# Who subtracts the low part of an expert's weights: VectorE with a GpSimd share, or VectorE alone

## The chip, the cores and the metric

The program runs on one core of a Trainium2 chip. Its engines are TensorE (matmuls, PE in the profile; its weight loads are PEld), VectorE (DVE), ScalarE (ACT), GpSimd (POOL) and SyncE (SP, which here only issues transfers). The metric is the device time of one execution in microseconds (us). A difference of about 0.3% (some 11 us) is what a measurement of this kernel can tell from no change.

## The reference

Two transformer blocks over 512 tokens of width 1024, all in fp32. The first block ends in a mixture of 32 experts, of which each token uses four:

```python
def expert_block(args):
    tok_b, e = args
    xb = h[tok_b]
    u = xb @ w1[e] + b1[e]                       # w1[e]: 1024 x 2048
    glu = jnp.minimum(u[:, 0::2], SWIGLU_LIMIT)
    lin = jnp.clip(u[:, 1::2], -SWIGLU_LIMIT, SWIGLU_LIMIT)
    act = glu * jax.nn.sigmoid(SWIGLU_ALPHA * glu) * (lin + 1.0)
    return act @ w2[e] + b2[e]                   # w2[e]: 1024 x 1024
```

All 32 experts' weights are read once: 32 x 12 MB. The second block (attention layers) takes the rest of the program and has no experts.

## The kernel before, in words

**The expert stage** takes the span from about 800 to 2390 us. An expert's weights are read in 24 pieces: 16 of `w1` (four column blocks of 512, by four pairs of row blocks) and 8 of `w2`. A piece `wraw` is 128 partitions x 1024 fp32 (two row blocks of 512 columns), 512 KB, loaded by one transfer that SP issues (L1312).

**Hi and lo.** A piece reaches TensorE in the type fp32r, as two parts that together keep fp32's precision: ScalarE copies it into `whi` as fp32r (L1324), and `wlo` = `wraw` - `whi` is the low part. The subtraction is divided by columns: of the 1024 columns VectorE does the first 736 (L1328) and GpSimd the last 288 (L1329); `q = 288` stands in `Weights.split`. Both need the finished `whi`, each reads two tensors in SBUF, and they need nothing of each other. Then TensorE uses both parts: for each of the two row blocks `x*hi` (L1706), `x*lo` (L1707) and, for blocks of 128 rows, `x_low*hi` (L1709). TensorE's L1707 waits until both engines have written their columns. The nine experts with a capacity of exactly 128 rows are not split (`whole(r)`): their pieces go to TensorE raw, as plain fp32 (L1702).

**Buffers.** There are seven `wraw` buffers and four of each of `whi` and `wlo`. A raw buffer comes free when ScalarE, VectorE and GpSimd have read it (or TensorE, of a whole expert), and SP then issues the next load into it, in order. `Weights.ahead` keeps the loads and splits ahead of `Weights.next`, which hands TensorE its next piece.

**What else runs on the two engines.** For each 512-column block of `w1` the function `swiglu` evicts the sums: for experts of 64 rows ScalarE copies half of them (L1717), VectorE adds the halves (L1718), clamps them (L1724, L1725), ScalarE makes the sigmoid (L1726), VectorE and GpSimd multiply (L1727, L1728), and TensorE transposes the result `ln` (L1687). GpSimd also issues the gathers of token rows (L1674), and close to the end of the stage multiplies the four accumulators by a gate (L1877, 128 x 1024 each), before VectorE adds the residual (L1878).

**The order.** Each engine runs its instructions in the order in which the program states them, and they wait for each other by semaphores. `order(g)` writes out by hand how the column blocks of three or four experts of different sizes follow each other.

**The other stages.** `split` serves the output projection before the experts with the same object. The second block makes a `Weights` object of its own (L3084).

Of the kernel before, what the change touches and what calls it, by code (L numbers as in the profile page):

```python
# [8 lines left out]
F = mybir.dt.float32  # L9
# [3 lines left out]
OP = mybir.AluOpType  # L13
# [85 lines left out]
class Blk1:  # L99
    def __init__(self, tc, ins, ctx, ident, ones, ps, dram):  # L100
        self.tc, self.nc, self.i, self.ps, self.dram = tc, tc.nc, ins, ps, dram
        self.ident, self.ones, self.ctx = ident, ones, ctx
        self.c = ctx.enter_context(tc.tile_pool(name="f1c", bufs=1, side="right"))
# [1150 lines left out]
def whole(r):  # L1254

    return CAP[r] == 128
# [32 lines left out]
class Rows:  # L1289


    def __init__(self, tiles, n, split):
        self.tiles, self.n, self.split = tiles, n, split


class Weights:


    def __init__(self, tc, ctx, raw=7, parts=4, kn=2, side="left"):
        self.tc, self.nc, self.kn = tc, tc.nc, kn  # L1300
        self.nraw, self.nsplit = raw, parts - 1
        self.raw = ctx.enter_context(tc.tile_pool(name="wraw", bufs=raw, side=side, reuse_waits="tile"))
        self.par = ctx.enter_context(tc.tile_pool(name="wpar", bufs=parts, side=side, reuse_waits="tile"))
# [12 lines left out]
    def split(self, raw, room=None):  # L1316
        nc = self.nc
        raw, n = raw
        hi, lo = room or [self.par.tile([128, self.kn, 512], R, name="w" + a) for a in ("hi", "lo")]
        if n < 512:  # L1320
            nc.scalar.activation(hi[:, :, :n], raw[:, :, :n], AF.Copy)
            nc.vector.tensor_tensor(lo[:, :, :n], raw[:, :, :n], hi[:, :, :n].bitcast(F), op=OP.subtract)
            return hi, lo
        nc.scalar.activation(hi, raw, AF.Copy)  # L1324
        q = 288
        rw, hw, lw = (t.rearrange("p k n -> p (k n)") for t in (raw, hi, lo))
        m = 512 * raw.shape[1] - q
        nc.vector.tensor_tensor(lw[:, :m], rw[:, :m], hw[:, :m].bitcast(F), op=OP.subtract)  # L1328
        nc.gpsimd.tensor_tensor(lw[:, m:], rw[:, m:], hw[:, m:].bitcast(F), op=OP.subtract)  # L1329
        return hi, lo  # L1330

    def stream(self, parts):
# [42 lines left out]
class Moe:  # L1375
# [301 lines left out]
    def rows_tiles(self, name, n, split=True, bufs=None):  # L1677
        m = 2 if n == 128 and split else 1
        return Rows([self.x.tile([128, 8, 128], R if split else F, name=name, tag=name, bufs=bufs or self.tbufs) for _ in range(m)], n, split)
# [104 lines left out]
    def experts(self, hD, x1, gt2):  # L1784
        nc, x_, c, I = self.nc, self.x, self.c, self.i
        self.tbufs, self.abufs, self.gbufs = 5, 6, 2
        kn = self.W.kn
        idxf, idx, gate, prepare = self.idxf, self.idx, self.gatec, self.prepare
        seq = sequence()
# [3 lines left out]
        def blocks(r):  # L1793
            return [(r, 0, min(CAP[r], 128))] + ([(32 + r, 128, 64)] if CAP[r] > 128 else [])
# [136 lines left out]
        for r in ranks:  # L1931
            m = sum(2 if b[2] == 128 and not whole(r) else 1 for b in blocks(r))
# [1176 lines left out]
```

## Time and profile before

| | us |
|---|---|
| median of 3 runs | 3789.82 (3784.77 to 3796.57) |
| the profiled execution, its own time | 3795.27 |
| its span, first to last instruction | 3793.5 |

| engine | busy in the whole span |
|---|---|
| PE | 3424.3 us, 90% |
| DVE | 2510.3 us, 66% |
| POOL | 1734.7 us, 46% |
| ACT | 1696.9 us, 45% |

The busy time of a matmul is modelled from its start, so a busy PE can still lose time. In the tables of waits, a row names the instruction that sat waiting, what ended its wait, the sum of such idle time, how often, and the longest. The granted clock is the share of TensorE's full 2.4 GHz: 1.00, or 0.50 (1.2 GHz) in stretches.

### The profile page before, as it was taken

The numbers are of one execution on the slowest core, as the hardware profiler recorded it, in microseconds if no ns is written. First come the engines' busy times: TensorE is split into PE (matmuls) and PEld (weight loads), VectorE is DVE, ScalarE is ACT, GpSimd is POOL, SyncE is SP. The second block draws the span as 40 slices with busy tenths as digits, with TensorE's granted clock in tenths as the row PEclk, the third lists the DMA queues.
The fourth block names the chain that finished last, engine by engine and source line by source line (L and its number), as shares of the span: only waits on it lengthen the run. The fifth ranks groups of instructions, "written<-read, shape, count | busy, mean of one in ns | idle before, by whom it ended". The sixth has DMA issues, their size and how long they took to land. (4 is left out here: it accounts for less than half of the span.)

```text
span 3793.5 us, 51274 instructions
## 1 busy us (share of the span) xinstructions
PE 3424.3 (90%) x16864; PEld 2510.5 (66%) x16864; DVE 2510.3 (66%) x4793; ACT 1696.9 (45%) x2937; POOL 1734.7 (46%) x1509
## 2 busy tenths in 40 slices
PE   7966679769898999999899989799999999999999
PEld 4756567645565565656465655488878878887887
DVE  7778875667786787766786856754566445546653
ACT  4634323224555555545555544444434434343442
POOL 4444333435665666555675755433342342334223
PEclk9976677869899999999999989899999999999999
DMA  7853243627778888877878788532221243223113
GB/s 255 265 141 83 65 104 92 211 98 249 248 234 276 290 285 279 263 263 262 295 258 294 239 273 290 174 90 75 74 85 51 61 140 101 79 73 84 40 51 106
DMA packets 420649, 653.86 MB, mean 172 GB/s; under 512 B 83939, under 2 KB 145568, under 8 KB 419862
## 3 DMA queue, kind: packets, MB, share of 16 engines
q1 hardware_dynamic: 414650, 633.32, 52.2%
q0 software_dynamic: 4000, 13.90, 1.2%
q10 hardware_dynamic: 1724, 3.28, 0.3%
q8 instruction: 135, 2.21, 0.2%
q14 instruction: 140, 1.15, 0.1%
HBM read 610.80 MB, written 39.61 MB: 171 GB/s over the span
## 5 line engine op out<-in xcount | busy, mean ns | idle before, releaser
L1329 POOL TENSOR_TENSOR wlo<-wraw,whi 128x288 fp32r<-128x288 f32 x736 | 957.3, 1311 | 1001.7 <-ACT whi L1324 935.2
L1328 DVE TENSOR_TENSOR wlo<-wraw,whi 128x736 fp32r<-128x736 f32 x736 | 828.5, 1133 | 472.4 <-ACT whi L1324 458.5
L1324 ACT ACTIVATE whi<-wraw 128x1024 fp32r<-128x1024 f32 x736 | 769.9, 1056 | 609.8 <-DMA wraw<-in_w 193.3
L2275 PE MATMUL psg<-whi,xh 128*128 128x512 f32 (+1 forms) x1152 | 472.4, 410 | 0.3 <-ACT xh L2292 0.3
L2277 PE MATMUL psg<-whi,xl 128*128 128x512 f32 (+1 forms) x1152 | 451.2, 392 | 0.0
L2276 PE MATMUL psg<-wlo,xh 128*128 128x512 f32 (+1 forms) x1152 | 449.7, 391 | 0.0
L1707 PE MATMUL ps<-wlo,x 128*128 128x512 f32 x928 | 383.7, 413 | 29.9 <-DVE wlo L1328 25.6
L1706 PE MATMUL ps<-whi,x 128*128 128x512 f32 x928 | 393.6, 424 | 1.0 <-ACT whi L1324 0.8
L1702 PE MATMUL ps<-wraw,x 128*128 128x512 f32 x576 | 277.4, 634 | 0.0
L2277 PEld LDWEIGHTS psg<-whi,xl 128*128 128x128 f32 x1152 | 217.5, 189 | 42.3
L1728 POOL TENSOR_TENSOR ln<-ln,sg 64x256 f32<-64x256 f32 (+1 forms) x152 | 166.5, 1096 | 163.9 <-DVE ln L1727 107.7
L2275 PEld LDWEIGHTS psg<-whi,xh 128*128 128x128 f32 x1152 | 218.1, 189 | 35.0 <-ACT xh L2292 1.5
L2276 PEld LDWEIGHTS psg<-wlo,xh 128*128 128x128 f32 x1152 | 218.3, 189 | 34.5
L1707 PEld LDWEIGHTS ps<-wlo,x 128*128 128x128 f32 x928 | 179.4, 193 | 91.9 <-DVE wlo L1328 44.7
L1706 PEld LDWEIGHTS ps<-whi,x 128*128 128x128 f32 x928 | 179.5, 193 | 72.1 <-issue 23.3
L1707 PE MATMUL ps<-wlo,a 128*128 128x512 f32 x464 | 195.8, 422 | 8.9 <-DVE wlo L1328 4.8
L1702 PEld LDWEIGHTS ps<-wraw,x 128*128 128x128 f32 x576 | 111.9, 201 | 136.2 <-issue 135.3
L1706 PE MATMUL ps<-whi,a 128*128 128x512 f32 x464 | 195.1, 421 | 1.5 <-ACT whi L1324 1.4
L2415 ACT ACTIVATE pexp<-pss,mx 128x128 f32<-128x128 f32 x192 | 101.0, 527 | 154.7 <-DVE mx L2410 66.6
L1726 ACT ACTIVATE sg<-gl 64x256 f32<-64x256 f32 (+1 forms) x152 | 62.9, 414 | 168.6 <-DVE gl L1724 153.6
L1702 PE MATMUL ps<-wraw,a 128*128 128x512 f32 x288 | 138.3, 619 | 0.0
L1707 PEld LDWEIGHTS ps<-wlo,a 128*128 128x128 f32 x464 | 90.6, 195 | 47.8 <-DVE wlo L1328 16.4
(736 smaller groups left out, 6927.8 us busy)
## 6 DMA issues: line engine op xcount, KB each, us to landing
wraw<-in_w SPq DMA_DIRECT2D x768, 512.0 KB
wraw<-in_w_in SPq DMA_DIRECT2D x140, 512.0 KB
mraw<-in_w_ada SPq DMA_DIRECT2D x32, 512.0 KB
wraw<-in_w_out SPq DMA_DIRECT2D x24, 512.0 KB
wada<-in_w_ada SPq DMA_DIRECT2D x16, 512.0 KB
wraw<-in_w_mem_kv SPq DMA_DIRECT2D x16, 512.0 KB
wraw<-in_w_branch_m SPq DMA_DIRECT2D x8, 512.0 KB
wraw<-in_w_branch_b SPq DMA_DIRECT2D x8, 512.0 KB
```

The source lines that it names most:

```text
L1324: nc.scalar.activation(hi, raw, AF.Copy)
L1328: nc.vector.tensor_tensor(lw[:, :m], rw[:, :m], hw[:, :m].bitcast(F), op=OP.subtract)
L1329: nc.gpsimd.tensor_tensor(lw[:, m:], rw[:, m:], hw[:, m:].bitcast(F), op=OP.subtract)
L1702: nc.tensor.matmul(ps, a, w[:, k], start=s, stop=e)
L1706: nc.tensor.matmul(ps, a, hi[:, k], start=s, stop=False)
L1707: nc.tensor.matmul(ps, a, lo[:, k], start=False, stop=e and not two)
L1726: nc.scalar.activation(sg[:m], gl[:m], AF.Sigmoid, scale=1.702)
L1728: nc.gpsimd.tensor_tensor(ln[:m], ln[:m], sg[:m], op=OP.mult)
L2275: nc.tensor.matmul(p, xh[:, kk], hi[:, k, :n], start=kk == 0, stop=False)
L2276: nc.tensor.matmul(p, xh[:, kk], lo[:, k, :n], start=False, stop=False)
L2277: nc.tensor.matmul(p, xl[:, kk], hi[:, k, :n], start=False, stop=kk == kch - 1)
L2415: nc.scalar.activation(p[:, :n], s[:, :n], AF.Exp, bias=nm, scale=-1.0, accum_out=H["d"][:, i:i + 1])
```

## The change

The 288 columns become an attribute of the class, and the expert stage sets it to zero for its own object. VectorE's instruction then covers all 1024 columns and GpSimd's is not issued. Everything else stays: the same loads, the same copy on ScalarE, the same matmuls. The output projection before it and the second block keep 288.

```diff
 class Weights:
+    share = 288
+
     def __init__(self, tc, ctx, raw=7, parts=4, kn=2, side="left"):
...
         nc.scalar.activation(hi, raw, AF.Copy)
-        q = 288
+        q = self.share
         rw, hw, lw = (t.rearrange("p k n -> p (k n)") for t in (raw, hi, lo))
         m = 512 * raw.shape[1] - q
         nc.vector.tensor_tensor(lw[:, :m], rw[:, :m], hw[:, :m].bitcast(F), op=OP.subtract)
-        nc.gpsimd.tensor_tensor(lw[:, m:], rw[:, m:], hw[:, m:].bitcast(F), op=OP.subtract)
+        if q:
+            nc.gpsimd.tensor_tensor(lw[:, m:], rw[:, m:], hw[:, m:].bitcast(F), op=OP.subtract)
         return hi, lo
...
     def experts(self, hD, x1, gt2):
         nc, x_, c, I = self.nc, self.x, self.c, self.i
         self.tbufs, self.abufs, self.gbufs = 5, 6, 2
+        self.W.share = 0
         kn = self.W.kn
```

## Rows read from the trace of the kernel before

**Rows 1.** The page, busy time and share of the span by engine.
```profile
PE 3424.3 (90%) x16864; PEld 2510.5 (66%) x16864; DVE 2510.3 (66%) x4793; ACT 1696.9 (45%) x2937; POOL 1734.7 (46%) x1509
```
**Rows 2.** Busy time by stretch: us, engines' busy (count), granted clock, DMA share, GB/s.
```profile
800.00:2390.00 1590.00, 1463.78 (x5296) 917.87 (x5296) 1142.34 (x1667) 828.20 (x1147) 948.06 (x772) 0.94 0.79 263
...
1300.00:1400.00 100.00, 89.41 (x301) 53.10 (x301) 74.65 (x94) 56.47 (x77) 65.08 (x52) 0.93 0.87 296
...
1473.00:1483.00 10.00, 9.42 (x16) 4.68 (x17) 5.12 (x11) 3.96 (x8) 2.84 (x4) 0.50 0.98 336
```
**Rows 3.** Waits of TensorE's matmuls, expert stage: sum us, times, longest us.
```profile
PE ps L1687 <- POOL ln L1728: 56.8, 19, 6.8
PE ps L1707 <- DVE wlo L1328: 30.4, 39, 3.5
PE ps L1687 <- DMA xg<-hD,idxi: 19.1, 7, 4.2
PE ps L1707 <- POOL wlo L1329: 7.0, 12, 1.1
```
**Rows 4.** Waits of TensorE's weight loads, same stage.
```profile
PEld ps L1707 <- DVE wlo L1328: 61.1, 77, 4.0
...
PEld ps L1707 <- POOL wlo L1329: 24.9, 47, 1.6
```
**Rows 5.** Groups by line and form, same stage: busy us, mean ns | idle before.
```profile
L1329 POOL TENSOR_TENSOR wlo<-wraw,whi 128x288 fp32r<-128x288 f32 x548 | 710.3, 1309 | 407.5 <-ACT whi L1324 376.0 <-PE ps L1707 9.8 <-PE ps L1702 7.8
L1328 DVE TENSOR_TENSOR wlo<-wraw,whi 128x736 fp32r<-128x736 f32 x548 | 621.7, 1144 | 273.6 <-ACT whi L1324 261.2 <-PE ps L1707 7.4 <-PE ps L1706 1.4
...
L1728 POOL TENSOR_TENSOR ln<-ln,sg 64x256 f32<-64x256 f32 x92 | 113.7, 1236 | 82.1 <-DVE ln L1727 44.0 <-PE ps L1702 19.7 <-PE ps L1707 4.2
...
L1724 DVE TENSOR_SCALAR gl<-us 64x256 f32<-64x256 f32 x92 | 54.0, 587 | 0.8
...
L1877 POOL TENSOR_TENSOR acc<-acc,gtr 128x1024 f32<-128x1024 f32 x4 | 11.4, 2847 | 0.0
...
L1878 DVE SCALAR_TENSOR_TENSOR acc<-x1t,acc 128x1024 f32<-128x1024 f32 x4 | 5.4, 1352 | 4.4 <-POOL acc L1877 2.3 <-DMA x1t<-x1D 2.1
```
**Rows 6.** Durations of the two subtractions, same stage: ns min/median/max, first and last start.
```profile
L1328 DVE TENSOR_TENSOR wlo<-wraw,whi x548: 903/926/3736, 824.1 to 2377.8; 128x736 fp32r<-128x736 f32 x183
...
L1329 POOL TENSOR_TENSOR wlo<-wraw,whi x548: 781/1487/6080, 824.2 to 2378.3; 128x288 fp32r<-128x288 f32 x183
```
**Rows 7.** Timeline, one split alone: start us, us, instruction xcount [idle before <-releaser].
```profile
1467.28 0.79 POOL L1329 TENSOR_TENSOR wlo<-wraw,whi 128x288 fp32r<-128x288 f32 x1 [6.88 <-ACT whi L1324]
1467.29 1.57 DVE L1328 TENSOR_TENSOR wlo<-wraw,whi 128x736 fp32r<-128x736 f32 x1 [7.60 <-ACT whi L1324]
```
**Rows 8.** Timeline, four splits behind each other ahead of an eviction.
```profile
1179.82 0.93 DVE L1328 TENSOR_TENSOR wlo<-wraw,whi 128x736 fp32r<-128x736 f32 x1 [4.73 <-ACT whi L1324]
1179.87 5.85 POOL L1329 TENSOR_TENSOR wlo<-wraw,whi 128x288 fp32r<-128x288 f32 x4 [2.50 <-ACT whi L1324]
...
1181.19 3.88 DVE L1328 TENSOR_TENSOR wlo<-wraw,whi 128x736 fp32r<-128x736 f32 x3 [0.45 <-PE ps L1707]
...
1185.70 0.28 DVE L1724 TENSOR_SCALAR gl<-us 64x256 f32<-64x256 f32 x1
```
**Rows 9.** Waits of SP's queue, the issuer of the loads, expert stage.
```profile
SPq L1312 <- DVE wlo L1328: 683.5, 469, 13.6
SPq L1312 <- POOL wlo L1329: 238.5, 345, 4.6
```
**Rows 10.** Waits of ScalarE, expert stage.
```profile
ACT whi L1324 <- DMA wraw<-in_w: 193.3, 148, 7.8
```
**Rows 11.** Timeline close to the stage's end, VectorE and GpSimd.
```profile
2323.66 1.23 DVE L1878 SCALAR_TENSOR_TENSOR acc<-x1t,acc 128x1024 f32<-128x1024 f32 x1
2323.81 3.27 POOL L1877 TENSOR_TENSOR acc<-acc,gtr 128x1024 f32<-128x1024 f32 x1
2324.81 3.06 DVE L1328 TENSOR_TENSOR wlo<-wraw,whi 128x736 fp32r<-128x736 f32 x1
```

## The prediction

> **What bounds the kernel now.** I read five views, in this order. First the page: TensorE is busy for 90% of the span [rows 1], so what does not free TensorE is worth nothing. Second, busy time by stretch, since the change touches one stage. In the expert stage, 1590 us of the span, TensorE is busy for 1463.8 us, VectorE for 1142.3 (72%), GpSimd for 948.1 (60%) and the DMA engines for 79%; the granted clock is 0.94 on average [rows 2]. So TensorE is the bound, with some 126 us of idle time and some slow clock. No other engine is full on average, but in single stretches the transfers are close: from 1300 to 1400 us they are 87% busy while TensorE has 89% [rows 2]. Third, TensorE's waits say what the 126 us are: 56.8 for the product `ln` that it is to transpose, 19.1 for gathered rows, and 30.4 + 7.0 = 37.4 us, in 51 waits, for `wlo` [rows 3]. Only these 37.4 us hang on the subtraction directly. TensorE's weight loads wait for it more often, 61.1 + 24.9 = 86.0 us in 124 waits [rows 4]; a load runs ahead of its matmul, so most of that is hidden, and it is the ceiling. Fourth, the two subtractions by form, then fifth their timeline, for what one costs.
>
> What the reader is to see there: the two engines hardly work side by side. VectorE's 736 columns take 926 ns in the median but 1144 on average; GpSimd's 288 take 781 at best, 1487 in the median, 1309 on average [rows 5, 6]. In the timeline of a single split both are ready together: GpSimd runs 0.79 us from 1467.28 and VectorE takes 1.57 instead of 0.93, ending at 1468.86, which is 0.79 us after GpSimd's end [rows 7]. Elsewhere VectorE starts first and takes its 0.93, and GpSimd's four take 5.85, 1.46 each [rows 8]. I read it so: while one of them reads its two tensors, the other makes no progress or little. The division by columns then buys no time: the pieces are worked off one behind the other, and `wlo` is complete 1.57 us after `whi` or later (1.57, or 0.93 + 0.78 = 1.71 when VectorE is first).
>
> **The change part by part.**
>
> *VectorE's instruction, 736 to 1024 columns.* No row shows this subtraction at 1024 columns. From below: VectorE's L1878 has the same width and two inputs in SBUF, and took 1.23 us in one instance [rows 11]. From above: its mean of 1.352 [rows 5]; the 926 ns scaled by 1024/736 give 1.288. I take 1.23, nearest in kind, and 1.35 as the other end. The addition is 1.23 - 0.93 = 0.30 us, x 548 = 164 us of VectorE's time.
>
> *GpSimd's instruction goes*: 548 of them, 710.3 us of its 948 [rows 5]. VectorE gets back what it spent blocked: (1144 - 926) ns x 548 = 119 us on this line alone, and on its other short operations: L1724 takes 0.28 us undisturbed [rows 8] and 587 ns on average, 92 x 0.31 = 28 us more [rows 5]. So VectorE's busy time changes by 164 - 119 - 28 = +17 us or, with the like on neighbouring lines that I have not priced, falls a little. 72% stays 72%.
>
> *When `wlo` is ready.* Alone: 1.23 us after `whi` in place of 1.57 (GpSimd first) or 1.71 (VectorE first), 0.34 or 0.48 earlier. In a queue of pieces the period falls from GpSimd's 1.46 to 1.23. At TensorE: 39 waits ended by VectorE x 0.34 = 13.3 us and 12 ended by GpSimd x 0.48 = 5.8 us (their mean is 0.58, so that fits into them): **-19 us**. The bounds: nothing, where the transfers feed the stage and an earlier `wlo` only meets the next late load; and 124 weight loads x 0.48 = 60 us, if each counted in full.
>
> *The clock.* Right behind the lo wait that ended at about 1473 us, from 1473 to 1483, the clock is 0.50, 1.2 of 2.4 GHz [rows 2]; ten such us do the work of five, so that wait cost 5 us more than itself. The longest lo wait is 3.5 us and the mean 0.7 [rows 3], so few are long enough to matter to it. I credit one such stretch, **-5 us**; bounds 0 and 15 (three).
>
> *The product `ln`, TensorE's largest wait.* It is at the end of a chain over ScalarE, VectorE and GpSimd. In the stretch at 1180 us VectorE's last three subtractions take 3.88 us; alone, 3 x 1.23 = 3.69, but the first of the four is 0.3 longer and may push them. So the eviction behind them comes 0.2 us earlier or not at all. GpSimd's L1728 is never queued behind a subtraction any more; where that set the moment it gains, and so does whatever part of its own 1.24 us [rows 5] is time shut out by VectorE, though VectorE's queue in front of it is no shorter. 19 waits x 0.1 = **-2 us**; bounds +6 and -12 (0.3 later; 0.6, half of the 1.24, earlier).
>
> *Close to the end*, GpSimd's four products of 128 x 1024 (L1877) take 2.85 us each [rows 5] and VectorE's subtraction behind one took 3.06 [rows 11]. With no GpSimd subtraction between them, they follow each other more closely and VectorE, whose instruction is now longer, can be shut out by the next: **+3 us**; bounds -3 (the excess of one such row gone twice over: 3.06 - 1.57 = 1.5 each) and 4 x 2.85 = +11 (each product once in full).
>
> *Loads.* SP waited 469 times for VectorE and 345 times for GpSimd before a load [rows 9]; a raw buffer now comes free some 0.3 us earlier, and no load is added. I price it at nothing: it can only bring loads forward. But it tells where part of the gain goes. ScalarE waited 148 times, 193.3 us, for a load to land [rows 10]; in such stretches (87% DMA, 296 GB/s) an earlier `wlo` counts once and not with each piece. I take 4 us off for it.
>
> The sum: -19 - 5 - 2 + 3 + 4 = -19 us. The profiled execution took 3795.3 us (span 3793.5 and 1.8 around it), which would become 3776; it lies 5.5 us above the median of the runs, so against that the forecast is 3789.8 - 19 = **3771 us**, 0.5% faster.
>
> A rule that speaks against this reading: the Trainium skill, "Perfetto Trace Analysis", section "Per-engine timelines" (GPSIMD Instruction), holds that a GpSimd instruction's span in a profile is not to be trusted and that the spacing of successive starts should be used. By the spacing here, four in 5.85 us, GpSimd's period is 1.46 [rows 8], near the median span of 1.487 [rows 6], so here the spans hold; if they did not, the sum would be that of the third case below.
>
> **The rivals.**
>
> *The gain is swallowed* (chance 0.22). The waits for `wlo` are replaced by waits for loads or for `ln`: the time lost is that of the transfers, at 79% over the stage and over 87% in its stretches. For it: ScalarE's 193 us. Against it: SP spent 922 us waiting for buffers [rows 9], so the transfers are mostly not what is late. The result would be 0 to -9 us, say 3785.
>
> *VectorE becomes the bound; slower* (0.10). Place: VectorE's queue in the expert stage. If the 218 ns over the median are not GpSimd's doing but stay, the instruction takes 1.144 + 0.30 = 1.44 us and VectorE is busy for 1142 + 164 = 1306 us, 82%. Each of the 39 waits that VectorE ends grows by 0.30 (+12 us; +23 with the 77 of the weight loads), the 19 waits for `ln` by as much (+6), the 7.0 us for GpSimd go: +11 to +22, and one or two stretches of slow clock at 5: some +20, 3810 us. It decides from a mean of about 1.45 us for the new instruction. Against it: the timeline, where the long instances are those beside GpSimd.
>
> *GpSimd's spans mislead* (0.08). Then only VectorE's rows count: its mean of 1.144 becomes 1.23, `wlo` is 0.09 later at 39 waits (+3 us) and the 7.0 us for GpSimd go: -4, within what can be measured, 3786.
>
> *The forecast* has 0.60, with a range of its own of -12 to -50 us (3740 to 3778), the far end being most of the 60 us.
>
> **How the numbers follow.** A change under 0.3%, 11 us, cannot be told from none. Faster: the forecast case, 0.60. Same: 0.22 + 0.08 = 0.30. Slower: 0.10. The range takes in the swallowed case and the end near zero of the slower one: 3740 to 3802.
>
> **What would show each step.** Right: VectorE's group at 128x1024 with a mean under 1.27 us and hardly any above 1.5; waits of TensorE for `wlo` halved from 37.4; GpSimd's L1728 at 64x256 well under its 1236 ns; VectorE's busy time in the stage within 30 us of 1142; TensorE's busy time the same. Wrong: a mean above 1.4 us; waits for `wlo` as long as before with ScalarE's waits for loads over 220 us (swallowed); more than 70 us of waits for `ln`; a granted clock below 0.93 in the stage.

## The result, and the profile after

The changed kernel takes 3734.63 us (3731.86 to 3742.22) against 3787.59 (3784.77 to 3796.57) for the kernel before on the same chip: a ratio of 0.986, 95% interval 0.984 to 0.988, or 53 us less. The forecast was 19 us less, 3771, with a range from 3740: the direction was right, and the gain was nearly three times as large.

Two statements made ahead of the prediction do not hold. First, the engines do not run their instructions in the order in which the program states them: the build chooses an order, and without GpSimd's subtractions it chose another one on the other engines too (251 of TensorE's 14162 matmuls stand in another place, 742 of VectorE's 4309 instructions). So the change did two things, and the first experiments part them.

Second, TensorE's L1707 does not always wait for both engines. A piece holds two row blocks of 512 columns side by side; the first row block lies wholly in VectorE's 736 columns, and its matmul starts when VectorE is done. In the timeline of the kernel before (start, us, instruction, idle before it) it starts at 2061.18, while GpSimd works on this piece until 2061.78:

```profile
2060.20 0.93 DVE L1328 TENSOR_TENSOR wlo<-wraw,whi 128x736 fp32r<-128x736 f32 x1 [1.30 <-ACT whi L1324]
2060.24 1.54 POOL L1329 TENSOR_TENSOR wlo<-wraw,whi 128x288 fp32r<-128x288 f32 x1 [0.67 <-ACT whi L1324]
2061.18 0.50 PE L1707 MATMUL ps<-wlo,a 128*128 128x512 f32 x1 [0.22 <-DVE wlo L1328]
```

In 22 of the 39 waits that VectorE ended, GpSimd was still subtracting when TensorE went on.

The line numbers are 2 to 3 higher than before (L1328 is now L1330, L1707 is L1710, L1728 is L1731). Busy time by engine, which answers to [rows 1]: only GpSimd has lost much, and TensorE's share has risen to 91%.

```profile
PE 3393.0 (91%) x16864; PEld 2514.0 (67%) x16864; DVE 2464.9 (66%) x4793; ACT 1698.0 (45%) x2937; POOL 1034.5 (28%) x957
```

The expert stage as one stretch (length, busy time and count of TensorE, weight loads, VectorE, ScalarE and GpSimd, granted clock, DMA share, GB/s), beside [rows 2]. Its last matmul on a split piece starts 59 us earlier (2321.2 against 2380.3 us), the clock is 0.96 where it was 0.94, and GpSimd is busy for 17% where it was for 60%:

```profile
800.00:2336.00 1536.00, 1431.17 (x5322) 919.16 (x5322) 1113.25 (x1709) 829.08 (x1147) 261.55 (x231) 0.96 0.81 272
```

The waits in that stretch (who waits, for what: sum in us, times, longest), beside [rows 3, 4, 9, 10]. TensorE's waits for `wlo` fall from 37.4 us to 14.5; those for `ln` and for gathered rows hardly move; SP's waits that end with a subtraction fall from 922 us to 495, but others took their place, and all its waits before a load together are 1086 us where they were 1117; and ScalarE waits less for loads, not more:

```profile
PE ps L1690 <- POOL ln L1731: 53.1, 19, 5.2
PE ps L1690 <- DMA xg<-hD,idxi: 18.8, 7, 5.3
PE ps L1710 <- DVE wlo L1330: 14.5, 20, 3.1
...
PEld ps L1710 <- DVE wlo L1330: 30.1, 42, 3.5
...
ACT whi L1326 <- DMA wraw<-in_w: 153.2, 137, 7.2
```
```profile
SPq L1314 <- DVE wlo L1330: 495.2, 325, 8.6
SPq L1314 <- PE ps L1705: 238.1, 108, 17.1
```

The groups by line and form (busy us, mean ns), beside [rows 5], and the durations of the subtraction (min/median/max), beside [rows 6]. The instruction at 1024 columns takes 1224 ns in the median and 1247 on average: without GpSimd's subtractions the mean lies 2% over the median, where it was 24% over it. L1727, an eviction of VectorE, falls from 587 to 295 ns. GpSimd's `ln` product, which should have become shorter, became longer (1236 to 1313): it takes 1623 ns on average where one of VectorE's subtractions runs beside it (57 times) and 807 where none does (35 times):

```profile
L1330 DVE TENSOR_TENSOR wlo<-wraw,whi 128x1024 fp32r<-128x1024 f32 x548 | 676.6, 1247 | 217.3 <-ACT whi L1326 205.5 <-PE ps L1710 5.7
...
L1731 POOL TENSOR_TENSOR ln<-ln,sg 64x256 f32<-64x256 f32 x92 | 120.8, 1313 | 491.6 <-DVE ln L1730 245.0 <-ACT sg L1729 105.2 <-PE ps L1705 90.7
...
L1727 DVE TENSOR_SCALAR gl<-us 64x256 f32<-64x256 f32 x92 | 27.1, 295 | 0.8
...
L1881 POOL TENSOR_TENSOR acc<-acc,gtr 128x1024 f32<-128x1024 f32 x4 | 10.9, 2733 | 11.2 <-DVE acc L1919 11.2
```
```profile
L1330 DVE TENSOR_TENSOR wlo<-wraw,whi x549: 1205/1224/3427, 829.1 to 2338.6; 128x1024 fp32r<-128x1024 f32 x183
```

**Where the 58 us of the span went.** I added up the stage from its first matmul on a split piece to its last: TensorE's idle gaps, and the time at a granted clock of 0.50. Of the latter about half is lost, where TensorE is busy in it (behind each other the matmuls start 0.43 us apart on split pieces and 0.85 on raw ones, against 0.235 and 0.43 at the full clock); idle time in it is counted as idle already. The stage shrinks from 1563.5 to 1498.0 us, 65.5 less (the span loses 7.5 less: 6.4 ahead of the stage and 1.1 behind it; what lies ahead of the stage is 814 to 823 us long over the fourteen kernels).

| | before | after | difference in time |
|---|---|---|---|
| waits for `wlo` | 37.4 | 14.5 | -22.9 |
| waits for `ln` | 56.8 | 53.1 | -3.7 |
| TensorE idle, all of it | 114.6 | 86.8 | -27.8 |
| us at clock 0.50 | 161.3 | 99.8 | |
| of these, TensorE busy | 132.8 | 88.9 | -22.0 (half of 43.9) |
| the rest of the stage | 1382.5 | 1366.7 | -15.8 |

The clock gave nearly as much as the waits for `wlo` themselves. Putting each slow stretch down to the longest wait from 6 us ahead of it up to its end: behind waits for `wlo` there were six, 47.8 us together (43.2 of them busy), and now two, 10.2 us (8.1 busy). Behind `ln` 63.0 busy us became 60.9; behind gathered rows 22.3 became 15.7. At half, that is -17.6, -1.1 and -3.3.

The rest is for the most part matmuls that start late without counting as idle. I took pairs of successive matmuls on split pieces at the full clock, their idle gaps taken off, and added up by how much their starts lie more than 0.233 us apart: 47.9 us before, 33.2 after, 14.7 less.

How one looks in the timeline of the kernel before (start, us, instruction, idle before it): up to the wait the matmuls start 0.23 to 0.34 us apart (those at 0.34 are the late ones), and behind 1.51 us of waiting 0.43 apart. This went on for 10.2 us, the stretch at 0.50 in [rows 2]. It is a wait of ordinary length:

```profile
1471.20 0.50 PE L1707 MATMUL ps<-wlo,x 128*128 128x512 f32 x1
1471.54 0.40 PE L1706 MATMUL ps<-whi,x 128*128 128x512 f32 x1
1473.45 0.80 PE L1707 MATMUL ps<-wlo,x 128*128 128x512 f32 x1 [1.51 <-DVE wlo L1328]
1474.04 0.63 PE L1706 MATMUL ps<-whi,x 128*128 128x512 f32 x1
1474.46 0.63 PE L1707 MATMUL ps<-wlo,x 128*128 128x512 f32 x1
```

### The profile page after: what moved, and what is told of

The parts are those of the page before. It is cut to its first block, busy times and chain, and to the rows that moved or that the text cites. A ratio compares the mean times of both kernels' runs of the same rounds, so it can differ in the third digit from the quotient of the medians.

```text
span 3735.5 us, 50031 instructions
## 1 busy us (share of the span) xinstructions
PE 3393.0 (91%) x16864; PEld 2514.0 (67%) x16864; DVE 2464.9 (66%) x4793; ACT 1698.0 (45%) x2937; POOL 1034.5 (28%) x957
## 5 line engine op out<-in xcount | busy, mean ns | idle before, releaser
L1330 DVE TENSOR_TENSOR wlo<-wraw,whi 128x1024 fp32r<-128x1024 f32 (+1 forms) x736 | 883.9, 1210 | 417.6 <-ACT whi L1326 404.3
L1326 ACT ACTIVATE whi<-wraw 128x1024 fp32r<-128x1024 f32 x736 | 769.9, 1057 | 616.2 <-DMA wraw<-in_w 153.2
L1731 POOL TENSOR_TENSOR ln<-ln,sg 64x256 f32<-64x256 f32 (+1 forms) x152 | 179.9, 1184 | 884.1 <-DVE ln L1730 464.3
L1332 POOL TENSOR_TENSOR wlo<-wraw,whi 128x288 fp32r<-128x288 f32 x184 | 241.4, 1313 | 591.8 <-ACT whi L1326 549.9
L1710 PE MATMUL ps<-wlo,x 128*128 128x512 f32 x928 | 373.9, 403 | 8.3 <-DVE wlo L1330 8.0
L2281 PEld LDWEIGHTS psg<-whi,xl 128*128 128x128 f32 x1152 | 217.9, 189 | 42.3
L1710 PEld LDWEIGHTS ps<-wlo,x 128*128 128x128 f32 x928 | 177.9, 192 | 50.1 <-DVE wlo L1330 15.2
L1710 PE MATMUL ps<-wlo,a 128*128 128x512 f32 x464 | 193.2, 417 | 6.6 <-DVE wlo L1330 6.6
L1677 POOL DMA_INDIRECT xg<-hD,idxi x38 | 40.4, 1062 | 288.7 <-PE ps L1690 271.2
L1710 PEld LDWEIGHTS ps<-wlo,a 128*128 128x128 f32 x464 | 90.6, 195 | 36.9 <-DVE wlo L1330 14.9
```

Source lines behind the costliest of these rows:

```text
L1677: self.last = nc.gpsimd.indirect_dma_start(out=x[:n], out_offset=None, in_=hD, in_offset=bass.IndirectOffsetOnAxis(ap=idx, axis=0))
L1710: nc.tensor.matmul(ps, a, lo[:, k], start=False, stop=e and not two)
L1731: nc.gpsimd.tensor_tensor(ln[:m], ln[:m], sg[:m], op=OP.mult)
L2281: nc.tensor.matmul(p, xl[:, kk], hi[:, k, :n], start=False, stop=kk == kch - 1)
```

## The experiments

All are timed beside the kernel before on the same chip (its medians there: 3785.7 for e1 to e4, 3791.4 for e5 to e8, 3783.3 for e9 to e12), so the ratio is the figure to compare. Idle, clock and waits are added up over the stage as above, from one profiled execution each (in brackets the us at 0.50 in which TensorE was busy); the last column is the mean of VectorE's subtraction.

| | us | ratio to before (95%) | idle | at 0.50 | `wlo` | `ln` | VectorE ns |
|---|---|---|---|---|---|---|---|
| before | 3787.6 | 1 | 114.6 | 161.3 (132.8) | 37.4 | 56.8 | 1144 at 736 |
| after | 3734.6 | 0.986 (0.984 to 0.988) | 86.8 | 99.8 (88.9) | 14.5 | 53.1 | 1247 |
| e1 alone, old order | 3727.7 | 0.985 (0.982 to 0.987) | 83.9 | 105.3 (87.2) | 14.7 | 50.7 | 1243 |
| e2 shared, new order | 3768.8 | 0.995 (0.993 to 0.997) | 112.1 | 138.0 (116.1) | 26.2 | 58.3 | 1156 at 736 |
| e3 lo later | 3816.9 | 1.008 (1.006 to 1.010) | 130.4 | 161.7 (131.4) | 53.7 | 56.6 | 1229 + 518 |
| e4 GpSimd reads | 3842.4 | 1.014 (1.011 to 1.017) | 158.3 | 198.6 (161.4) | 41.5 | 92.2 | 1420 |
| e5 fill | 3738.2 | 0.986 (0.984 to 0.989) | 39.7 | 30.6 (27.1) | 17.3 | 2.1 | 1243 |
| e6 GpSimd writes | 3743.6 | 0.987 (0.984 to 0.990) | 93.2 | 108.6 (89.5) | 19.6 | 56.6 | 1243 |
| e7 `ln` on VectorE | 3719.0 | 0.981 (0.978 to 0.984) | 74.7 | 91.3 (80.3) | 13.2 | 35.5 | 1219 |
| e8 zero everywhere | 3732.7 | 0.984 (0.981 to 0.988) | 90.2 | 109.4 (92.8) | 16.7 | 54.3 | 1244 |
| e9 fill, half | 3703.2 | 0.978 (0.976 to 0.980) | 43.3 | 42.3 (38.8) | 14.8 | 8.5 | 1244 |
| e10 e7 and fill | 3689.7 | 0.976 (0.974 to 0.977) | 43.0 | 41.6 (41.0) | 11.8 | 6.0 | 1220 |
| e11 share 144 | 3750.3 | 0.992 (0.989 to 0.994) | 96.6 | 113.1 (95.4) | 19.3 | 54.3 | 1184 at 880 |
| e12 share 432 | 3808.6 | 1.006 (1.005 to 1.008) | 133.4 | 157.6 (125.0) | 47.3 | 59.4 | 1202 at 592 |

**e1 and e2: the order, or who subtracts?** Each engine's order is held by edges between neighbours on that engine, which cost no semaphore: e1 is the changed kernel in the order of the kernel before, e2 the shared subtraction in the order of the changed kernel.

```diff
+        for p, n in zip(line, line[1:]):      # the engine's wanted order
+            tc.add_manual_dep(n, p.name, how, reason="order")
```

> The build does not keep the program's order of instructions: it ordered 251 of TensorE's 14162 matmuls, 742 of VectorE's 4309 instructions and 288 of ScalarE's 2718 differently once the share was zero. This kernel has VectorE subtract all 1024 columns as in the change, with every engine's instructions held in the order of the kernel before. Theory A (the two subtractions shut each other out, so wlo was late; the order is a by-product): 3735 to 3750 us, waits of TensorE for wlo near 15 us, slow clock as short as in the changed kernel. Theory B (the new order made the gain): 3775 to 3795 us.

> The mirror of the first: GpSimd keeps its 288 columns as before, and every other instruction is held in the order of the changed kernel. Theory A: 3775 to 3800 us, VectorE's 736 columns at a mean of 1.14 us or more, waits for wlo near 37 us. Theory B: 3735 to 3750 us.

e1 has the whole gain. The order alone, with the share kept, is worth 0.5% (17 us by the medians; of the 13.1 us by which the profiled stage is shorter, 8.4 came at the clock, half of 132.8 - 116.1). So e2 came out under its 3775 to 3800, with 26.2 us of waits for `wlo` in place of the 37 expected. Once VectorE subtracts alone, the order is worth nothing any more: old and new cannot be told apart (0.985 and 0.986). So it is the share. In e2 VectorE's 736 columns still take 1156 ns on average (two groups by form of e2):

```profile
L1329 POOL TENSOR_TENSOR wlo<-wraw,whi 128x288 fp32r<-128x288 f32 x540 | 694.9, 1300 | 404.2 <-ACT whi L1324 365.4 <-PE ps L1707 12.1 <-PE ps L1702 9.4
L1328 DVE TENSOR_TENSOR wlo<-wraw,whi 128x736 fp32r<-128x736 f32 x540 | 619.0, 1156 | 250.7 <-ACT whi L1324 240.8 <-PE ps L1707 5.9 <-PE ps L1706 0.7
```

**e3: the low part later, without GpSimd.** VectorE does the last 288 columns a second time, which was to make `wlo` complete about 0.5 us later. The order is that of the changed kernel in e3 to e6.

```diff
         if q: ...
+        else:
+            nc.vector.tensor_tensor(lw[:, m-288:], rw[:, m-288:], hw[:, m-288:].bitcast(F), op=OP.subtract)
```

> The changed kernel in its own order, and behind each whole subtraction VectorE subtracts the last 288 columns once more (same values). No GpSimd in it; wlo is ready some 0.45 us later, 1.7 us after whi, about as in the kernel before. Theory A with its second half (what counts is when wlo is ready, and the clock falls behind the waits for it): back to 3775 to 3800 us, waits for wlo of 35 us or more, slow clock as long as before. Theory C (the gain comes from GpSimd's absence as such: other instructions of VectorE, the evictions and the product ln, run faster without it): 3735 to 3755 us.

The groups by form, TensorE's waits and one of them in the timeline of e3: the second subtraction takes 0.52 us, so VectorE needs 1.75 us for a piece, and the time is 0.8% over before's, beyond the 3800 expected. The delay is not where it was meant to be. 50.9 of the 53.7 us of waits end with the first subtraction, and in all 65 of these TensorE goes on before the second is done, since the first row block has none of its columns. What comes late is the next piece in VectorE's queue: 57 of all waits for `wlo`, 44.7 us, end with a subtraction that VectorE came to straight from other work. So a longer stay of each piece on VectorE makes the loss without GpSimd; e3 does not test a late second half by itself, and VectorE's other work had 284 us more in the queue with it as well.

```profile
L1328 DVE TENSOR_TENSOR wlo<-wraw,whi 128x1024 fp32r<-128x1024 f32 x548 | 673.3, 1229 | 117.9 <-ACT whi L1324 115.8 <-PE ps L1706 0.9
L1331 DVE TENSOR_TENSOR wlo<-wraw,whi 128x288 fp32r<-128x288 f32 x548 | 284.0, 518 | 18.8
```
```profile
PE ps L1711 <- DVE wlo L1328: 50.9, 65, 3.5
...
PE ps L1711 <- DVE wlo L1331: 2.8, 15, 0.4
```
```profile
926.10 1.72 DVE L1328 TENSOR_TENSOR wlo<-wraw,whi 128x1024 fp32r<-128x1024 f32 x1
927.85 0.46 DVE L1331 TENSOR_TENSOR wlo<-wraw,whi 128x288 fp32r<-128x288 f32 x1
927.87 0.79 PE L1711 MATMUL ps<-wlo,x 128*128 128x512 f32 x1 [1.39 <-DVE wlo L1328]
```

**e4 and e6: what of GpSimd holds VectorE up?** In e4 GpSimd does its old subtraction beside VectorE's whole one, into a tile that nobody reads, so that TensorE does not wait for it (the buffers do: 334.6 us of SP's waits before a load end with it). In e6 it writes zeros there instead, at the same places of its queue, and reads nothing (544 pieces in both, all but the first few). But the writes have nothing to wait for, so they run in bursts: in e6 163 of VectorE's 548 subtractions had a write beside them, in e4 479 of 540 a reading.

```diff
         if q: ...
+        elif self.scr is not None:            # e4
+            nc.gpsimd.tensor_tensor(self.scr[:, :288], rw[:, m-288:], hw[:, m-288:].bitcast(F), op=OP.subtract)
+        elif self.scr is not None:            # e6, in its place
+            nc.gpsimd.memset(self.scr, 0.0)
```

> The changed kernel in its own order, and GpSimd again reads the last 288 columns of each piece and its whi and writes the difference into a tile that nobody reads; TensorE waits for VectorE alone. Theory A: VectorE's instruction is shut out as before, mean 1.45 us or more; wlo later than in the changed kernel; 3765 to 3800 us. Theory D (what went away is the second writer that TensorE and the loads waited for, not the contention): 3735 to 3745 us, VectorE's mean near 1.25.

> The changed kernel with an extra instruction of GpSimd per piece that nobody awaits, as in e4_gpsimd_reads and at the same place of its queue, but which reads nothing in SBUF: it writes zeros, 128x512, into a tile that is not read. Theory (VectorE is shut out by GpSimd's reading of SBUF, as the Trainium skill's SBUF page has it): VectorE's subtraction at 128x1024 has a mean of 1.23-1.28 us, as in the changed kernel, and the time is 3735-3755 (GpSimd's own products come later by up to 0.5 us each). Rival (any work of GpSimd on SBUF, writing too, or its queue, holds VectorE up): a mean of 1.35 or more, time over 3780.

The groups of the two subtractions in e4, and of VectorE's subtraction and GpSimd's write in e6:

```profile
L1329 DVE TENSOR_TENSOR wlo<-wraw,whi 128x1024 fp32r<-128x1024 f32 x548 | 769.7, 1420 | 202.6 <-ACT whi L1325 196.9 <-PE ps L1709 1.8 <-issue 0.5
L1331 POOL TENSOR_TENSOR oh<-wraw,whi 128x288 f32<-128x288 f32 x544 | 868.2, 1596 | 324.0 <-ACT whi L1325 268.8 <-issue 15.9 <-POOL oh L1331 6.9
```
```profile
L1329 DVE TENSOR_TENSOR wlo<-wraw,whi 128x1024 fp32r<-128x1024 f32 x548 | 673.7, 1243 | 215.4 <-ACT whi L1325 203.6 <-PE ps L1709 6.5 <-PE ps L1689 0.5
L1331 POOL MEMSET oh<- 128x512 f32 x544 | 287.2, 528 | 22.4
```

VectorE's subtractions one by one, by what GpSimd did beside them:

| GpSimd beside it | times | mean ns | longest |
|---|---|---|---|
| e6, nothing | 289 | 1220 | 1229 |
| e6, a write alone, running at its start | 100 | 1219 | 1229 |
| e4, a reading alone, begun after it | 143 | 1224 | 1230 |
| e4, a reading alone, running at its start | 249 | 1496 | 1843 |

So it is GpSimd's reading that holds VectorE up, and only where GpSimd began first; its writing does not. This agrees with the Trainium skill, "SBUF — State Buffer", section "Who interferes with whom": an instruction of VectorE with two inputs in SBUF contends with GpSimd's reads, not with its writes, and the order of issue decides which of the two is blocked.

As a whole e4 takes 2.8% more than the changed kernel (3842 against 3735), more than the 3800 expected, while VectorE's mean of 1420 stays under the 1450 ns expected. Not all of this is VectorE's delay: of 71.5 us more idle time on TensorE 39 are waits for `ln`, whose product stands in GpSimd's longer queue, and 27 are waits for `wlo`. The time of e6 cannot be told from the changed kernel's.

**e11 and e12: other shares,** 144 and 432 columns, in the order of the changed kernel (`self.W.share = 144`, `= 432`).

> The changed kernel's order held, with a GpSimd share of 144 columns of 1024 (VectorE 880). Theory (the two subtractions go one behind the other, so that the parts add): VectorE alone some 1.08 us and GpSimd's 144 columns some 0.4 us, `wlo` after about 1.5 us, halfway between 1.23 (no share) and 1.71 (288): about halfway between 3735 and 3769, 3745-3760. Rival (they work side by side and the parts only need balance): at or under the changed kernel's time, 3725-3735.

> The same with 432 columns for GpSimd (VectorE 592): VectorE alone some 0.77 us and GpSimd 1.17 us. Theory (one behind the other): `wlo` after 1.94 us, 0.23 later than with 288: 3780-3800, and VectorE's mean at 592 columns well over its shortest 0.77. Rival (side by side): `wlo` after 1.2 us, as with no share, 3730-3745.

With e2 between them, the time rises with the share throughout: 0.986, 0.992, 0.995, 1.006 for 0, 144, 288 and 432 columns, and the waits for `wlo` go 14.5, 19.3, 26.2, 47.3. In the pieces at which both engines stood free, `wlo` is complete 1.46, 1.62 and 1.79 us after `whi` with 144, 288 and 432 columns (medians), where VectorE alone takes 1.26 with none. At none of these shares are two engines better than one. At 432 columns it came out a little above the 3800 expected. VectorE's group in e12 shows 1202 ns for 592 columns, nearly what it needs for all 1024 alone:

```profile
L1329 POOL TENSOR_TENSOR wlo<-wraw,whi 128x432 fp32r<-128x432 f32 x545 | 808.5, 1498 | 351.3 <-ACT whi L1324 312.2 <-PE ps L1702 24.1 <-PE ps L1707 6.8
L1328 DVE TENSOR_TENSOR wlo<-wraw,whi 128x592 fp32r<-128x592 f32 x545 | 649.6, 1202 | 229.2 <-ACT whi L1324 215.9 <-PE ps L1707 9.5 <-POOL wlo L1329 1.6
```

**e5 and e9: does the clock fall because TensorE stands idle?** TensorE gets matmuls that compute nothing, just ahead of the transposes that waited longest for `ln`. They take away no wait of the work, and they delay what follows if they overrun. The added lines (e5 with 512 columns, at 17 places; e9 with 256, at 18):

```diff
+        for _ in range(FILL.get(self.nln, 0)):
+            nc.tensor.matmul(p[:, :256], self.ident, self.iota[:, :256], start=True, stop=True)
         for k in range(n):
             nc.tensor.transpose(p[:, k * m:(k + 1) * m], src[:m, k * 128:(k + 1) * 128], self.ident[:m, :m])
```

> The changed kernel with each engine's order held, and 97 extra fp32 matmuls of TensorE (identity by a constant, 128x512, about 0.43 us each, overwritten by what follows) put ahead of those 17 groups of transposes of `ln` that TensorE waited over 1 us for in the changed kernel: they fill some 85% of these waits, 42 us, with matmuls that compute nothing. They take away no wait of the work itself. Theory (the clock falls because TensorE stands idle, and a us of wait costs more than itself): the granted clock of the expert stage rises from 0.96 to 0.98, us at 0.50 fall from about 100 to 40-65, and the time falls to 3705-3725, though TensorE has 42 us more to do. Rival (the clock follows something else, such as the load of the whole stage, and the 31 us that the change gained at the clock have another cause): us at 0.50 stay at 90-110, time 3730-3745; where the extra matmuls overrun the waits, up to 3755.

> As e5_warm, but each extra matmul has half the columns (128x256): in e5_warm one took 0.91 us in two passes (194 rows, 88.6 us) where 0.43 had been put, so that it overran the waits by some 42 us. Here 102 of them, some 46 us, fill about 85% of the waits for `ln` of the changed kernel. Theory (idle TensorE lowers the clock, and that is where 31 of the 53 us came from): us at 0.50 in the expert stage fall from 100 to 30-50, waits that are left for `ln` are under 15 us, and the time is 25-35 us under the changed kernel's: 3700-3715, by doing 46 us of useless work. Rival (what e5_warm gained at the clock came from its overrun, a fuller TensorE, and not from the filled waits): us at 0.50 over 80, time 3730-3745.

In e5 the clock did what the theory says, more than expected (30.6 us at 0.50 for 99.8), and the time did not, since each filler took twice what I had put: the group of e5 shows two rows per matmul, 194 in all, 88.6 us where I meant 42. That 88.6 us of useless work left the time where it was (0.986 for both kernels; the profiled stage is 9.6 us longer) is itself the finding: 47 fell into idle time and 31 came back at the clock (half of the 61.8 us less that TensorE was busy at 0.50). e9, with half the columns, has 49.3 us of fill:

```profile
L1690 PE MATMUL ps<-miota,ident 128*128 128x512 f32 x194 | 88.6, 606 | 0.0
```
```profile
L1690 PE MATMUL ps<-miota,ident 128*128 128x256 f32 x204 | 49.3, 392 | 0.0
```

One place of the changed kernel, in its timeline and by windows of 10 us (columns as above; the clock is the third number from the end): TensorE waits 4.06 us for `ln`, then starts matmuls 0.43 apart, and 5.12 us more a little later. The clock is 0.66, 0.78, 0.88:

```profile
1159.23 0.65 PE L1690 MATMUL ps<-ident,ln 128*128 128x128 f32 x4
1163.94 0.69 PE L1690 MATMUL ps<-ident,ln 128*128 128x128 f32 x2 [4.06 <-POOL ln L1731]
...
1166.30 0.63 PE L1709 MATMUL ps<-whi,x 128*128 128x512 f32 x1
1166.72 0.63 PE L1710 MATMUL ps<-wlo,x 128*128 128x512 f32 x1
...
1175.94 0.47 PE L1690 MATMUL ps<-ident,ln 64*128 64x64 f32 x2 [5.12 <-POOL ln L1731]
```
```profile
1160.00:1170.00 10.00, 6.06 (x17) 4.36 (x18) 4.72 (x8) 4.41 (x8) 1.78 (x2) 0.66 0.93 320
1170.00:1180.00 10.00, 4.88 (x15) 3.51 (x14) 5.10 (x8) 2.99 (x5) 0.72 (x1) 0.78 0.64 214
1180.00:1190.00 10.00, 10.00 (x40) 8.02 (x39) 4.80 (x5) 5.33 (x6) 0.00 (x0) 0.88 0.37 108
```

The same part of e9, the timeline of the second of the two places and the same windows. Fillers fill the wait but for 0.88 us, the matmuls behind it start 0.23 apart, and the clock is 1.00 throughout:

```profile
1155.32 4.48 PE L1690 MATMUL ps<-miota,ident 128*128 128x256 f32 x20
1160.68 0.33 PE L1693 MATMUL ps<-ident,ln 64*128 64x64 f32 x2 [0.88 <-POOL ln L1735]
...
1161.28 0.40 PE L1714 MATMUL ps<-wlo,a 128*128 128x512 f32 x1
1161.51 0.40 PE L1716 MATMUL ps<-whi,a 128*128 128x512 f32 x1
```
```profile
1160.00:1170.00 10.00, 9.32 (x41) 7.53 (x42) 3.59 (x4) 3.81 (x5) 0.62 (x1) 1.00 0.54 178
1170.00:1180.00 10.00, 10.00 (x33) 5.95 (x32) 8.17 (x10) 7.56 (x10) 0.00 (x0) 1.00 0.74 249
1180.00:1190.00 10.00, 10.00 (x42) 7.68 (x41) 8.08 (x9) 7.28 (x8) 0.00 (x0) 1.00 0.99 343
```

e9 is faster than the changed kernel (0.978 against 0.986, intervals apart) by doing 49 us of nothing. Over the stage that is 43.5 us of idle time filled, and 50.1 us less of TensorE busy at 0.50, of which half, 25.1, is gained; 43.5 + 25.1 - 49.3 = 19.3, and the stage is 20.3 us shorter. That TensorE's idling lowers its clock, and what that costs at these waits for `ln`, is thereby shown and not only argued. For the waits for `wlo` it is carried over: nobody filled those.

**e7, e8 and e10.** e7 puts GpSimd's remaining elementwise work of the stage on VectorE as well; e8 sets the share to zero in the whole program (`share = 0` in the class); e10 is e7 with its order held and 68 fillers at its 13 longest waits for `ln`.

```diff
-        nc.gpsimd.tensor_tensor(ln[:m], ln[:m], sg[:m], op=OP.mult)
+        nc.vector.tensor_tensor(ln[:m], ln[:m], sg[:m], op=OP.mult)
...
-                nc.gpsimd.tensor_tensor(a, a, fin["gt"], op=OP.mult)
+                nc.vector.tensor_tensor(a, a, fin["gt"], op=OP.mult)
```

> The changed kernel with the rest of GpSimd's elementwise work of the expert stage on VectorE too: the product `ln` (64x256, 1.31 us on GpSimd in the changed kernel) and the four products by the gate near the end (128x1024, 2.85 us each before). VectorE gets some 30 us more to do. Theory (what TensorE waits for comes earlier where no two engines read SBUF beside each other; each us of wait costs some 1.7 us with the clock behind it): waits for `ln` fall from 53 to about 35 us, since the product takes 0.3-0.5 us in place of 1.3 at 19 places; with the clock 25-30 us less: 3705-3715. Rival (VectorE's queue is what sets `ln`, so that the product is only late on another engine): waits for `ln` 50 or more, 3730-3740.

> The changed kernel with GpSimd's share at zero in the output projection before the experts and in the second block as well. Theory (the share holds VectorE up wherever both subtract, but it costs time only where TensorE waits for the low part): the projection and the second block wait little for it, 3715-3735. Rival (there VectorE is fuller and the share does relieve it): 3745 or more.

> e7_ln_vector (no elementwise work on GpSimd in the expert stage) with its order held and 68 extra matmuls of TensorE (128x256, about 0.46 us, 31 us) ahead of the 13 groups of transposes that waited over 0.8 us for `ln` in e7_ln_vector. Theory: the two gains add, us at 0.50 from 91 to 30-50, time 20-30 us under e7_ln_vector's 3719: 3690-3700. Rival (the slow clock left in e7_ln_vector hangs on other places, as its first 400 us with a clock of 0.91): us at 0.50 over 70, 3705-3720.

In e7 the `ln` product on VectorE takes 411 ns in the median (its durations below, min/median/max), a third of GpSimd's 1313 on average at 64x256, and TensorE's waits for it fall to 35.5 us (its row of the waits). The time is 0.981, against 0.986 for the changed kernel, with intervals that touch; it stays some 4 us above the 3715 expected, since of the 18 us less for `ln` only 12 remained of idle time (74.7 against 86.8), and the clock gave 4 us (half of 8.6).

```profile
L1728 DVE TENSOR_TENSOR ln<-ln,sg x152: 403/411/478, 838.2 to 2292.2; 64x256 f32<-64x256 f32 x92, 128x256 f32<-128x256 f32 x60
```
```profile
PE ps L1687 <- DVE ln L1728: 35.5, 14, 4.6
```

In e8 the rest of the program gains nothing that can be told from the changed kernel in the time, as expected. In its profiled execution what lies behind the stage takes 1404 us, in the other kernels 1408 to 1414, so the second block may gain a few us there. e10 is the fastest: 3689.7 us, 2.4% under the kernel before and 0.5% under e7 (0.976 and 0.981, intervals apart).

## Why the prediction was wrong in its size

By its own steps:

- *VectorE's instruction at 1024 columns*: 1.23 us was taken; the median is 1.224, the mean 1.247. Right. VectorE's busy time was to change by +17 us or fall a little: over the span it fell by 45 us (2510.3 to 2464.9), since its other short operations gained as well.
- *The waits for `wlo`*: -19 was put, and -22.9 came. The reading of [rows 7, 8], that the two subtractions are worked off one behind the other, holds: e1, e4, e11 and e12 bear it out, and e6 shows the cause. How it becomes time at TensorE was only half right. The sum takes 0.34 us off each of the 39 waits that VectorE ended, as if GpSimd were first every time. Of 193 pieces at which both engines stood free, VectorE was first in 171: it was done 0.96 us after `whi` (median) and GpSimd 1.62. So the first row block, which needs VectorE alone, now comes later there (1.26), and only the second earlier. What fell are the waits for a subtraction that VectorE came to straight from other work, 21.5 us to 8.6, by the shorter queue; those where it had stood free went from 8.9 to 6.0, and GpSimd's 7.0 went. That the sum of these came close to -19 is in part luck.
- *The clock* is the step that failed. It said of the waits for `wlo` that "few are long enough to matter to it" and credited one stretch, -5 us with a bound of 15. The stretches behind such waits were six, 47.8 us, and two are left, 10.2 us: -17.6 us by the time in which TensorE was busy in them. Behind waits for `ln` and for gathered rows 4.4 us went as well. All together -22.0 us, where -5 had been taken. I had looked at one stretch instead of adding up all time at 0.50 beside the waits ahead of it. TensorE's busy time, which was to stay the same, fell from 3424.3 to 3393.0 us, which fits fewer matmuls at 0.50.
- *The weight loads* were left out: 86.0 us of waits, "most of that is hidden", and nothing in the sum. They fell to 30.1 us, and matmuls that start late without an idle gap gave 14.7 us. That these late starts come from late weight loads was not tested.
- *The product `ln`*: -2 was put, -3.7 came, but the argument under it fell. L1728 did not get shorter when GpSimd lost its subtractions: it took 1313 ns, not 1236, since it is VectorE that shuts it out (1623 ns beside one of VectorE's subtractions, 807 without). e7 gives the price of leaving it on GpSimd, with the four products near the end: some 16 us, by intervals that touch.
- *Close to the end* (+3) and *swallowed by the transfers* (+4): neither came. GpSimd's four products take 2.73 us where they took 2.85; ScalarE waits 40 us less for loads (193.3 to 153.2), so the gain was not swallowed there. The sum with -22.0 at the clock and without these two terms is -43; with the late starts it is -58. The stage lost 65.5, of which 7.5 came back outside it.
- *The rivals*: "VectorE becomes the bound" needed a mean of 1.45 us; 1.247 was measured. e4, at 1420, where `ln` comes later too, is slower than before by 1.4%. That GpSimd's spans mislead is excluded by the times.

What stays open: what makes the matmuls start late, and why the order alone moves the clock by 23 us of slow time with the same idle time (114.6 and 112.1 in the kernel before and in e2). The clock depends on where the waits fall, not on their sum alone: over the kernels without fillers TensorE is busy at 0.50 for 0.9 to 1.2 us for each us that it is idle, so that a us of waiting costs 1.5 to 1.6 us in all, the late starts not counted.

## What to carry to other kernels

Before an instruction with two inputs in SBUF is divided between VectorE and GpSimd, compare its shortest duration with its mean in the kernel: 926 against 1144 ns told here that the engines shut each other out, and the whole on VectorE was faster at every share tried. Where TensorE is the bound, price a wait by itself and by the clock behind it: add up the time at the lower clock over the stage, without what is idle in it, and see which waits stand ahead of it. Look which columns a matmul reads before a wait is put down to the whole tile. And look up the order in which the build has put the instructions, of both kernels, before a gain is put down to one edit.

## What was not expected of the hardware

- In the kernel before, four waits of TensorE for `wlo` of only 1.2 to 1.6 us (2.1 to 2.9 us with the other gaps from 6 us ahead of the slow stretch up to its end) had 6.8 to 10.2 us at 1.2 GHz behind them; and matmuls that compute nothing, put into longer waits, brought TensorE back to 2.4 GHz and made the run shorter (0.978 of the kernel before's time against 0.986, e9).
- An fp32 matmul of 128x512, which the profile shows as two rows, costs 0.91 us, not the 0.43 of the earlier estimate: 194 rows for 97 instructions, 88.6 us (e5).
- A subtraction of VectorE that began while GpSimd was writing (128x512, e6) took 1219 ns on average, no more than the 1220 with GpSimd still; one that began while GpSimd was reading (128x288 from two tensors, e4) took 1496.
